# Pair 14's second product moved into the last first product, the last SwiGLU by halves, the softmax's VectorE operations pinned in program order

## The chip, the core and the metric

The kernel runs on one core of one Trainium2 chip, as one launch. The core has TensorE (PE: matmuls and transposes, with its weight loads listed as PEld), VectorE (DVE), ScalarE (ACT), GpSimd (POOL) and SyncE (SP), which here issues nearly all loads. The metric is the device time of one execution in microseconds; a lower one is better. [...]

## What is computed

One encoder block on 256 positions of 1024 columns, in float32. The first half (adaLN modulation, gated delta rule, short convolution, output projection) is untouched by the change. The second half is a mixture of 32 experts, four for each token, and a final RMSNorm:

```
h = rmsnorm(x, norm2_w) * (1 + sc_f) + sh_f
logits = h @ router_w + router_b
top_val, top_idx = lax.top_k(logits, 4);  gates = softmax(top_val)
for each expert e, on the tokens that chose it:
    gate, up = split(x_blk @ w1[e] + b1[e])            # 1024 -> 2 * 1024
    act = min(gate, 7) * sigmoid(1.702 * gate) * (clip(up, -7, 7) + 1)
    y = act @ w2[e] + b2[e]                            # 1024 -> 1024
x = x + gt_f * sum over the four experts of gates * y
out = rmsnorm(x, final_norm_w)
```

## The kernel before

**Routing.** The logits `lg` of 128 tokens by two halves go through VectorE: `max` and `match_replace` give the selection `sel` (copied four times wide into `sel4`). Three small matmuls of TensorE count, for every token, its rank among an expert's tokens; `rk` (L1280) is made of them, and `slots_of(0)` (L1312) turns `rk` into the 0/1 matrix `P` of the first four experts. `gather_part` multiplies `P` with the normalised tokens (`h2h` and `h2l`, two parts of one number) and writes the experts' inputs, `XT`, 128 columns at a time. `busy(n)` issues matmuls whose result nobody reads. `route_counts()`, called behind the first product of pair 0 in the program, makes `sel4`, the counts and the order of the other 28 experts, and the softmax of the gates (`nmx`, `ex`, `den`, `gat`, L1492 to L1498).

**The stream of experts.** The 32 experts are taken as 8 groups of four, and each group as two pairs: pairs 0 to 15. The first product of a pair (`w1_pair`) has eight chunks k0 to k7; a chunk is two loads of 1 MB (one for each expert of the pair) and 16 matmuls, in four column quarters c of 512 into four PSUM banks: c = 0, 1 are the gate's halves, c = 2, 3 the up's. Profile rows count each such matmul as two records, so a chunk is 32 of them. `swiglu(128, pss[half], pss[2 + half])` works on quarters (0, 2), then on (1, 3): g = min, tanh on ScalarE, u = clip, and two fused operations on VectorE; the tile `g` has two buffers, `u` and `th` one each. `to_ff` turns its result by eight transposes and two ScalarE copies into `aT`. The second product is a `Second` object with four blocks of the same size (two loads of 1 MB, 32 records), and `end()`: VectorE scales the two PSUM banks into `ysb`, and two `combine` calls, each of two matmuls, add the rows back to the tokens' `x1`.

Pair p's loop step runs its first product, and then the four blocks of pair p - 1 with `turn(p)`, the transposes of pair p, among them. The combines of pair p - 1 run within the first product of pair p + 1. In the last step (p = 15) blocks 0 and 1 of pair 14 run inside the first product, behind k2 and k4, and blocks 2 and 3 behind k7. Then come the combines of pair 14 and the second product of pair 15 in another shape, `w2_cols`: columns 0 to 767 in four steps (loads of 768 KB), the first parts of the final norm, and columns 768 to 1023. `xf`, `square` and `finish_part` are the final RMSNorm.

**Order.** A scheduler puts each engine's instructions in order by a simulated timeline. Instructions marked `pin(...)` (`tc.keep_in_program_order`) keep their order in the program among the pinned ones of their engine; all of the expert stage's matmuls and transposes are pinned (`held[0]`). The weight loads go through one ring of 18 half-slots of 1 MB (`w_half`); six chunks of pair 0 and three of pair 1 are loaded ahead, k6 and k7 of pair 0 into tiles that are free till later (`pre`). SP issues a load when the half-slot is released by the matmuls that read it.

## Time and profile before

| | us |
|---|---|
| median of 3 runs | 1378.63 (1376.73 to 1378.85) |
| the profiled execution, its own time | 1378.51 |
| its span, first to last instruction | 1376.7 |
| TensorE busy | 1268.5 (92%) |
| VectorE busy | 516.8 (38%) |
| ScalarE busy | 282.2 (21%) |

The profile's page gives busy time and shares over the whole span; the stages differ, so the rows below take them apart. A timeline row gives the start, the time, the engine, the line, the operation with output and inputs, the count of merged instructions, and in brackets the idle time of the engine before it with what ended that. The chain that the page follows back from the end reaches only to 1367.9 us, where the runtime branch for overflowing experts ends, and so it says nothing of the stages ahead of that.

### The profile page before, as it was taken

Reading aid. Unit: us, or ns where it says so; the run is one execution under the profiler, and the core shown is the slowest. Engines: PE = TensorE matmul, PEld = TensorE weight load, DVE = VectorE, ACT = ScalarE, POOL = GpSimd, SP = SyncE. Lnnn points to the kernel's source line nnn. Section 1 sums busy time; section 2 is a strip of 40 time slices with the busy share of each in tenths; the row PEclk is TensorE's granted clock in tenths of the full one; section 3 lists DMA queues with packets and bytes.
Section 4 is the critical chain, followed back from the end, with each engine's and each line's share of the span. In section 5 each row is a group of like instructions: output and inputs, shape, how many; then the busy total and the mean of one; then the engine's idle time right before and its main releaser. Section 6 shows DMA issues by size and latency. Waiting matters only on the chain. (4 is left out here: it accounts for less than half of the span.)

```text
span 1376.7 us, 24562 instructions
## 1 busy us (share of the span) xinstructions
PE 1268.5 (92%) x10276; PEld 666.0 (48%) x10277; DVE 516.8 (38%) x1018; ACT 282.2 (21%) x546; POOL 151.9 (11%) x126
## 2 busy tenths in 40 slices
PE   6999998899999999999999898988989898898986
PEld 4888897899996333223333233322322332232322
DVE  3387879965773321232122112122211212211113
ACT  3455562554642010101001001000100100010001
POOL 4555785000100000000000000000000000000000
PEclk9999999999999999999999999999999999999998
DMA  9978977246697899999999999999999999999994
GB/s 338 309 234 270 309 234 239 77 146 251 224 369 291 365 421 421 414 421 421 421 420 421 421 420 421 420 421 421 420 421 421 420 420 421 421 420 421 421 400 172
DMA packets 132533, 492.69 MB, mean 358 GB/s; under 512 B 10942, under 2 KB 66623, under 8 KB 84801
## 3 DMA queue, kind: packets, MB, share of 16 engines
q1 hardware_dynamic: 128176, 485.95, 89.4%
q10 hardware_dynamic: 4241, 5.12, 1.1%
q8 instruction: 82, 1.34, 0.4%
q14 instruction: 34, 0.28, 0.1%
HBM read 486.82 MB, written 4.21 MB: 357 GB/s over the span
## 5 line engine op out<-in xcount | busy, mean ns | idle before, releaser
L1303 PE MATMUL acc<-wst,XT 128*32 128x512 f32 x4088 | 474.9, 596 | 24.3 <-DMA wst<-in_moe_w_dram 24.3
L1303 PEld LDWEIGHTS acc<-wst,XT 128*32 128x32 f32 x4088 | 133.0, 110 | 339.4 <-issue 281.7
L1303 PE MATMUL acc<-wst,aT 128*32 128x512 f32 (+1 forms) x2112 | 250.5, 585 | 25.6 <-DMA wst<-in_moe_w_dram 25.6
L313 PE MATMUL mm<-hh,wl 128*128 128x256 f32 (+1 forms) x520 | 149.9, 289 | 6.2 <-DVE wl L263 3.7
L1303 PEld LDWEIGHTS acc<-wst,aT 128*32 128x32 f32 x2112 | 70.5, 110 | 175.8 <-issue 113.3
L311 PE MATMUL mm<-hh,wh 128*128 128x256 f32 (+1 forms) x520 | 151.7, 292 | 1.2 <-DVE cacc L556 1.2
L312 PE MATMUL mm<-hl,wh 128*128 128x256 f32 (+1 forms) x520 | 149.9, 288 | 0.0
L262 ACT CAST wh<-raw 128x1024 fp32r<-128x1024 f32 (+1 forms) x89 | 91.9, 1039 | 95.1 <-PE mm L312 52.2
L1360 DVE TENSOR_SCALAR g<-acc 128x512 f32<-128x512 f32 x32 | 22.1, 692 | 229.8 <-PE acc L1303 229.5
L88 POOL TENSOR_TENSOR rs<-ss,half_m 128x2 f32<-128x2 f32 x3 | 2.1, 701 | 949.6 <-DVE ss L1752 884.9
L311 PEld LDWEIGHTS mm<-hh,wh 128*128 128x128 f32 (+1 forms) x520 | 100.6, 194 | 12.6 <-issue 8.3
L313 PEld LDWEIGHTS mm<-hh,wl 128*128 128x128 f32 (+1 forms) x520 | 100.5, 193 | 8.6 <-DVE wl L263 3.9
L312 PEld LDWEIGHTS mm<-hl,wh 128*128 128x128 f32 (+1 forms) x520 | 100.7, 194 | 0.9 <-issue 0.8
L263 POOL TENSOR_TENSOR wl<-raw,wh 128x1024 fp32r<-128x1024 f32 x36 | 88.5, 2468 | 71.3 <-ACT wh L262 64.3
L1361 ACT ACTIVATE th<-g 128x512 f32<-128x512 f32 x32 | 20.2, 630 | 362.6 <-DVE g L1360 297.4
L1407 DVE TENSOR_TENSOR x<-x,misc 128x512 f32<-128x512 f32 (+1 forms) x66 | 44.3, 672 | 124.8 <-PE misc L1303 124.8
L1414 DVE TENSOR_TENSOR ysb<-acc,gtf 128x512 f32<-128x512 f32 (+1 forms) x33 | 22.2, 675 | 137.1 <-PE acc L1303 137.1
L263 DVE TENSOR_TENSOR wl<-raw,wh 128x1024 fp32r<-128x1024 f32 (+1 forms) x53 | 64.0, 1212 | 24.0 <-ACT wh L262 23.9
L1303 PE MATMUL misc<-ysb,pgT 128*128 128x512 f32 (+1 forms) x132 | 64.0, 606 | 1.8 <-DVE ysb L1414 1.0
L1332 DVE TENSOR_SCALAR XT<-misc,afc,mod 128x256 f32<-128x256 f32 x32 | 17.4, 544 | 127.1 <-PE misc L1303 127.1
L1303 PE MATMUL misc<-P,h2h 128*128 128x256 f32 x128 | 39.6, 332 | 20.5 <-ACT XT L1334 18.4
L1303 PEld LDWEIGHTS misc<-P,h2h 128*128 128x128 f32 x128 | 24.0, 187 | 53.2 <-issue 27.5
(390 smaller groups left out, 1384.9 us busy)
## 6 DMA issues: line engine op xcount, KB each, us to landing
wst<-in_moe_w_dram SPq DMA_DIRECT2D x372, 1024.0 KB, 19.8
raw<-in_w_in_dram SPq DMA_DIRECT2D x36, 1024.0 KB, 7.4
raw<-in_ada_w_dram SPq DMA_DIRECT2D x24, 1024.0 KB, 9.6
wst<-in_moe_w_dram SPq DMA_DIRECT2D x8, 768.0 KB, 19.0
raw<-in_w_out_sc_dram SPq DMA_DIRECT2D x4, 1024.0 KB, 5.2
raw<-in_w_up_a_dram SPq DMA_DIRECT2D x4, 1024.0 KB, 8.6
raw<-in_w_o_dram SPq DMA_DIRECT2D x4, 1024.0 KB, 10.2
wst<-in_moe_w_dram SPq DMA_DIRECT2D x16, 256.0 KB, 6.6
```

The lines of the kernel that those rows point to most:

```text
L88: G.tensor_tensor(dst, src, half_m.to_broadcast([128, n]), op=OP.pow)
L262: a = A.copy(wh, src)
L263: b = (V if job.lo == "v" else G).tensor_tensor(wl, src, wh.bitcast(FT), op=OP.subtract)
L311: PE.matmul(ps, wh[:, k, :], ah[:, k, :], start=k == 0, stop=False, skip_group_check=True)
L312: PE.matmul(ps, wh[:, k, :], al[:, k, :], start=False, stop=False, skip_group_check=True)
L313: PE.matmul(ps, wl[:, k, :], ah[:, k, :], start=False, stop=k == KT - 1, skip_group_check=True)
L1303: return held[0](PE.matmul(*a, **kw))
L1332: V.tensor_scalar(xq[:, k], o, afc[:, k:k + 1], mod[:, 24 + k:25 + k], op0=OP.mult, op1=OP.add)
L1360: V.tensor_scalar(g[:n], g_ps[:n], 7.0, None, op0=OP.min)
L1361: A.activation(th[:n], g[:n], AF.Tanh, scale=0.851)
L1407: V.tensor_tensor(xv, xv, p[:, 0:n], op=OP.add)
L1414: V.tensor_tensor(y, ps[:, 0:n], gtf_box[0][:, c0:c0 + n], op=OP.mult)
```

## The change

Four edits. The column quarters of every first product run in the order 0, 2, 1, 3. Five kinds of VectorE operations of `route_counts` (the copies of `sel4`, the two products with the sum for `den`, the reciprocal, the two for `gat`) are pinned. In the last step, all four blocks of pair 14 run inside the first product, behind k2, k3, k4 and k5; its scaling follows block 3, and its two combines stand behind k6. `to_ff` can do one half, so that pair 15's first half is turned ahead of `w2_cols` and its second half behind the first column step.

```diff
-            for c in range(4):
+            for c in (0, 2, 1, 3):
                 for j in range(4):
                     mm(pss[c][j * 32:(j + 1) * 32], xq[:, k, (4 * pa + j) * 32:(4 * pa + j + 1) * 32],
...
-    def to_ff(gs):
-        aT = work.tile([128, KT, 128], FT, name="aT", tag="aT", bufs=2)
-        for half in range(2):
+    def to_ff(gs, aT=None, halves=(0, 1)):
+        if aT is None:
+            aT = work.tile([128, KT, 128], FT, name="aT", tag="aT", bufs=2)
+        for half in halves:
...
-            V.tensor_copy(sel4[:, t, 1:4], sel4[:, t, 0:1].to_broadcast([128, 3, NE]))
+            pin(V.tensor_copy(sel4[:, t, 1:4], sel4[:, t, 0:1].to_broadcast([128, 3, NE])))
...
-            V.scalar_tensor_tensor(ex[:, t], ex[:, t], 1.0, sel[:, t], op0=OP.mult, op1=OP.mult,
-                                   accum_out=den[:, t:t + 1])
-        V.reciprocal(den, den)
+            pin(V.scalar_tensor_tensor(ex[:, t], ex[:, t], 1.0, sel[:, t], op0=OP.mult, op1=OP.mult,
+                                       accum_out=den[:, t:t + 1]))
+        pin(V.reciprocal(den, den))
         for t in range(2):
-            V.tensor_scalar(gat[:, t], ex[:, t, None, :].to_broadcast([128, 4, NE]), den[:, t:t + 1], None, op0=OP.mult)
+            pin(V.tensor_scalar(gat[:, t], ex[:, t, None, :].to_broadcast([128, 4, NE]), den[:, t:t + 1], None,
+                                op0=OP.mult))
...
-        done = 0
         if p == NP - 1:
 
             box = []
-            for done, k in enumerate((2, 4)):
-                at[k].append(lambda c=done: (box or box.append(second(p - 1)) or box)[0].block(c))
-            done += 1
+            at[2].append(lambda: box.append(second(p - 1)))
+            for c in range(4):
+                at[2 + c].append(lambda c=c: box[0].block(c))
+            at[5].append(lambda: box.extend(box[0].end()))
+            at[6] += [lambda h=h: box[1 + h]() for h in range(2)]
         first_product(p, at)
...
-        if p:
+        if 0 < p < NP - 1:
...
-            at[3 if done else 2].append(lambda: turn(p))
-            sp = box[0] if done else second(p - 1)
-            for c in range(done, 4):
+            at[2].append(lambda: turn(p))
+            sp = second(p - 1)
+            for c in range(4):
...
-    last = (aTs[NP - 1], gts[NQ - 1], regs[NQ - 1])
-    sums[NP - 2][0]()
-    w2_cols(NP - 1, PARTS[0:2], *last, {0: [sums[NP - 2][1]]})
+    last = (to_ff(gs[NP - 1], None, (0,)), gts[NQ - 1], regs[NQ - 1])
+    w2_cols(NP - 1, PARTS[0:2], *last, {0: [lambda: to_ff(gs[NP - 1], last[0], (1,))]})
```

## Rows read from the trace of the kernel before

**Rows 1.** Windows: length, busy us (instructions) by engine, clock, DMA share, GB/s.
```profile
439.30:441.80 2.50, 2.50 (x24) 1.08 (x24) 0.00 (x0) 0.56 (x1) 0.00 (x0) 1.00 0.35 79
...
471.60:476.80 5.20, 5.20 (x52) 1.56 (x48) 2.31 (x11) 0.00 (x0) 0.00 (x0) 1.00 0.21 54
476.80:1338.00 861.20, 790.49 (x6332) 262.84 (x6324) 187.92 (x396) 59.12 (x102) 0.10 (x1) 1.00 1.01 420
```

**Rows 2.** Timeline of VectorE, routing.
```profile
429.23 0.41 DVE L1474 COPY sel<-sel 128x96 f32<-128x96 f32 x2
430.77 0.19 DVE L1494 SCALAR_TENSOR_TENSOR ex<-ex,sel 128x32 f32<-128x32 f32 x1 [1.13 <-ACT ex L1493]
...
431.81 0.22 DVE L1280 SCALAR_TENSOR_TENSOR rk<-misc,sel 128x64 f32<-128x64 f32 x1
432.13 0.76 DVE L1312 TENSOR_TENSOR P<-iota,rk 128x256 fp32r<-128x256 f32 x2
432.81 2.46 DVE L1214 SCALAR_TENSOR_TENSOR h2l<-x,rs,h2h 128x256 fp32r<-128x256 f32 x6
...
444.59 0.54 DVE L1332 TENSOR_SCALAR XT<-misc,afc,mod 128x256 f32<-128x256 f32 x1 [8.86 <-PE misc L1303]
```

**Rows 3.** Timeline of TensorE, routing and the start of pair 0.
```profile
429.20 0.39 PE L1277 MATMUL misc<-sel,tri_s 128*128 128x32 f32 x2
429.42 1.14 PE L1185 MATMUL mm<-one_f,ident 128*128 128x128 f32 x8
432.71 0.36 PE L1303 MATMUL misc<-P,h2h 128*128 128x256 f32 x1 [2.15 <-DVE P L1312]
...
434.46 5.17 PE L1303 MATMUL acc<-wst,XT 128*32 128x512 f32 x32
...
440.24 3.64 PE L1303 MATMUL acc<-wst,XT 128*32 128x512 f32 x32
```

**Rows 4.** Windows, columns as in rows 1: the first chunk of pair 0.
```profile
434.40:437.70 3.30, 3.30 (x17) 0.79 (x20) 1.33 (x4) 0.00 (x0) 0.00 (x0) 0.51 1.02 393
```

**Rows 5.** Timeline of SP's queue: weight issues near pairs 0 and 1.
```profile
439.68 0.84 SPq L968 DMA_DIRECT2D wst<-in_moe_w_dram  x2
...
474.62 4.24 SPq L1428 DMA_DIRECT2D wst<-in_moe_w_dram  x4
```

**Rows 6.** Timeline of TensorE, from the last first product's k7.
```profile
1328.10 3.20 PE L1303 MATMUL acc<-wst,XT 128*32 128x512 f32 x26 [1.34 <-DMA wst<-in_moe_w_dram]
...
1333.09 3.64 PE L1303 MATMUL acc<-wst,aT 128*32 128x512 f32 x32 [0.51 <-DMA wst<-in_moe_w_dram]
1338.05 3.62 PE L1303 MATMUL acc<-wst,aT 128*32 128x512 f32 x26 [1.32 <-DMA wst<-in_moe_w_dram]
1341.60 1.22 PE L1306 MATMUL misc<-ident,g 128*128 128x128 f32 x8
1343.03 1.98 PE L1303 MATMUL misc<-ysb,pgT 128*128 128x512 f32 x4 [0.21 <-ACT aT L1398]
1344.95 2.79 PE L1303 MATMUL acc<-wst,aT 128*32 128x512 f32 x32
...
1349.58 7.95 PE L1303 MATMUL acc<-wst,aT 128*32 128x512 f32 x96
```

**Rows 7.** Timeline of VectorE and ScalarE: the last SwiGLU and `aT`.
```profile
1329.20 0.69 DVE L1360 TENSOR_SCALAR g<-acc 128x512 f32<-128x512 f32 x1 [35.28 <-PE acc L1303]
...
1330.92 0.69 DVE L1362 TENSOR_SCALAR u<-acc 128x512 f32<-128x512 f32 x1 [0.17 <-PE acc L1303]
...
1332.44 0.69 DVE L1364 SCALAR_TENSOR_TENSOR g<-th,g 128x512 f32<-128x512 f32 x1
...
1342.38 1.09 ACT L1398 ACTIVATE aT<-misc 128x512 f32<-128x512 f32 x2 [8.53 <-PE misc L1306]
```

**Rows 8.** Timeline of TensorE: two longer waits within the stream.
```profile
906.53 3.64 PE L1303 MATMUL acc<-wst,aT 128*32 128x512 f32 x32 [1.78 <-DMA wst<-in_moe_w_dram]
...
1031.82 5.15 PE L1303 MATMUL acc<-wst,aT 128*32 128x512 f32 x28 [2.42 <-DMA wst<-in_moe_w_dram]
```

## The prediction

> **What bounds the kernel now.** I read the windows by stage first, then the timelines of the two places that the change touches, and last the waits of TensorE. In the windows [rows 1] the reader is to see three facts. From 476.8 us to 1338 us the DMA engines are full at 420 GB/s while TensorE is busy 790 of 861 us: the weight stream sets the pace there, and TensorE work that moves about inside this stretch is worth nothing. Just ahead of it the stream twice runs dry, from 439.3 to 441.8 us and from 471.6 to 476.8 us (DMA share 0.35 and 0.21) with TensorE at 100%. By the code the ring of 18 half-slots is then full of weights (six chunks of pair 0, three of pair 1), and SP can issue only when TensorE has finished a chunk. So whatever starts pair 0 sooner moves the whole stream. After 1338.05 us no matmul waits for a weight any more (the tail, below): the rest of the kernel is a chain of TensorE, VectorE and ScalarE, which sets the end.

> **Routing: the held operations.** The timeline of VectorE [rows 2] shows what stands ahead of pair 0. The rank counts for `rk` leave TensorE at 429.20 + 0.39 = 429.59 us [rows 3], but `rk` starts at 431.81 us. Ahead of it VectorE copies `sel4` (from 429.23 us), then stands 1.13 us for ScalarE's exponentials, then does the softmax from 430.77 us. None of that is needed by `rk`, `P` or the gather; it is needed by the matmuls after pair 0. TensorE stands 2.15 us for `P` [rows 3]. The change pins those operations, which puts them behind `P` and the `h2l` columns that are pinned ahead of them. Then `rk` can start when its counts are there, which I take at 0.2 us after 429.59, an estimate from the 0.2 us between `P`'s first half, half of 0.76 us from 432.13 on, and the gather at 432.71. With the row's spacings, `rk` to `P` 0.32 us and `P` to gather 0.58 us, the gather starts at 429.79 + 0.32 + 0.58 = 430.69 us and not at 432.71: 2.02 us sooner. It can't be sooner than the end of the warm-up matmuls, 429.42 + 1.14 = 430.56 [rows 3], so 2.15 is the upper bound. The lower bound is nothing, if other work slips into VectorE's freed place.

> The held operations, seven instructions and two accumulator reads, take 0.41 us for `sel4` and about 1.04 us for the softmax [rows 2]. I cost them at nothing: behind `P` come `h2l` (2.46 us), then they, then the second `XT` eviction (0.54), done at about 430.86 + 2.46 + 1.45 + 0.54 = 435.3 us. What waits for it is the second chunk of pair 0, which would start near 436.7. So 1.4 us of cover; past that, each us late is a us on TensorE. After that VectorE stands 8.86 us [rows 2].

> **Routing: the clock.** [...] The first chunk of pair 0 therefore takes 5.17 us where the next takes 3.64 [rows 3]. With the gap gone I take it at 3.64: another 1.53 us. Bounds: 0 (the clock falls all the same) to 1.53.

> **What becomes of these 3.55 us.** SP's first issue of the stage, at 439.68 us, waits for that first chunk; the one at 474.62 us waits for the first chunk of pair 1 [rows 5]. With TensorE 3.55 us sooner, the first issue comes at 436.1, while the earlier transfers still run (to 439.3): the first dry stretch goes. The second starts some 2 us sooner for it and ends 3.55 us sooner, with TensorE's release. From there the full stream [rows 1] and all behind it run 3.55 us ahead. These us can only be lost again after the last weight of the stream.

> **The tail.** Moved are blocks 1 to 3 of pair 14's second product (six 1 MB loads and 96 matmul records): block 1 from behind k4 to behind k3, blocks 2 and 3 from behind k7 to behind k4 and k5. On SP, k4's loads come behind block 1's, and those of k6 and k7 behind blocks 2 and 3. Twelve chunks of 2 MB go ahead of pair 15's second-product weights either way, so the eleventh and the twelfth still land when they do now, at 1333.09 and 1338.05 [rows 6], only they are k6 and k7 and no longer blocks 2 and 3. No queue but SP's is passed, and SP's other waits don't change, the ring being as deep.

> From 1333.09 us on I count TensorE's work. Now: two blocks, eight transposes, two combines, four column steps, ending at 1349.58 + 7.95 = 1357.53 [rows 6]: 24.44 us, of which it stands 1.32 (for the weights) and 0.21 us. Afterwards: k6, two combines, k7, four transposes, one column step, four transposes, three column steps. A chunk of either product is 32 records of 3.64 us, so it is the same work, and only the idle time differs. The combines take 1.92 us each (1343.03 to 1344.95): k7 starts at 1333.09 + 3.55 + 3.84 = 1340.5, after its weights, so the 1.32 us go. (With k7 at 1338.05 the combines would have been free; they are not.)

> What comes instead is the last SwiGLU, which today runs under blocks 2 and 3 and afterwards has nothing over it but k7 itself. With S the start of k7, today's rows give the first half's `g` at S + 1.10 and the third quarter's `u` at S + 2.82, 0.86 us a quarter [rows 6, 7]. In the order 0, 2, 1, 3 the first half's `u` is in the second quarter: S + 1.96. From `u` to the end of its last operation is 1332.44 + 0.69 - 1330.92 = 2.21 us, so half 0 is ready at S + 4.17; its transposes start near S + 4.25, where k7 ended at S + 3.55: 0.70 us idle. ScalarE starts 0.78 us after the transposes (1341.60 to 1342.38) and takes 0.55, so the first column step starts near S + 5.75; less 0.61 us of transposes that is 0.87 us idle. Half 1, four more operations of about 0.7 us, is ready near S + 7.0, under that step. New idle 1.57 us against 1.53: **the tail comes out even, at +0.04 us.** Bounds: -1.53 (no idle at all), and +0.86 if VectorE takes the second `g` ahead of the two operations that finish half 0.

> The quarters' new order in the other pairs, 4 x 4 matmuls either way, costs and brings nothing: their SwiGLU ends long before its transposes, under the full stream.

> [...] The row at 1031.82 us shows TensorE after 2.42 us without work at the lower clock, 5.15 us for 28 records; after 1.78 us at 906.53 it kept 3.64 [rows 8]. In the new tail it would stand 0.70 and 0.87 us with four transposes between. [...]

> **Sum.** -2.02 - 1.53 + 0.04 = -3.51 us. The profiled execution took 1378.51 us with a span of 1376.7, so 1375.0; the median of the runs is 0.12 us above it: **1375.1 us**, 0.26% less. About 0.2% (2.8 us) is what a measurement of this kernel can tell from no change.

> **Rivals.** (1) *The clock falls in pair 0 all the same.* For it: the small matmuls from 428 to 430.6 us stay. Against: the only standstill there is gone. 1376.6 us. [...] (3) *Combines and SwiGLU both hide:* 1373.6. Against: the times of k7 above. (4) *Slower: the last SwiGLU stands bare.* If VectorE does both halves before TensorE gets the first, the transposes wait till S + 7.1 in place of 4.25: +2.85 us, and as after the shorter gaps of [rows 3, 8] the clock falls: +1.53. Net +0.87 us, 1379.5. It decides from 3.51 us of extra time on. For it: `g`, `u`, `th` are few buffers, and today VectorE does both `g` first [rows 7]. Against: today the second `g` is ready ahead of the first `u`; in the new order it isn't.

> **Chances.** Forecast 0.54, (1) 0.14, (2) 0.17, (3) 0.06, (4) 0.09. Faster than by 0.2% means under 1375.9: most of the forecast (0.47, since runs spread over 2 us), all of (3), a little of (1) and (2): 0.56. Slower by 0.2%, over 1381.4, is only the worst of (4) or something that I don't see: 0.07. Within: 0.37. The range goes from (3) with some spread, 1372.9, to (2) with the second `g` first and spread, 1378.6; above lies (4).

> **What would show it.** Gather near 430.7 us; the first chunk of pair 0 in 3.6 us at full clock; no dry stretch near 440; k7 of pair 15 starting some 2.4 us after its weights; two short idle times before the first column step, together near 1.6 us, and the clock through them. It is wrong if `rk` still waits for something on VectorE, if the clock falls in either place, or if the end of the stream doesn't move with pair 0.

## The result and the profile after

The changed kernel takes 1385.32 us (median of 5 runs, 1383.42 to 1387.48), the kernel before 1377.57 us (5 runs, 1376.73 to 1378.85): a ratio of 1.0054, 95% interval 1.0042 to 1.0067. The forecast was 1375.1 us, 0.26% less; it came out 0.54% more. The profiled execution took 1385.25 us with a span of 1383.4, 6.7 us above the span before.

Where are they? The first place to look is TensorE's waits between 424 and 560 us, each with its sum, count and longest in us. Of the changed kernel:

```profile
PE misc L1303 <- DVE sel L1475: 4.5, 1, 4.5
PE misc L1303 <- ACT XT L1334: 2.6, 4, 0.7
PE misc L1303 <- DVE P L1312: 2.1, 1, 2.1
```

The second and third are the waits of before: the one for `P`, which was to go, is still 2.1 us. The first is new. VectorE's timeline of the changed kernel shows both reasons:

```profile
426.55 0.15 DVE L1493 TENSOR_SCALAR nmx<-mx 128x1 f32<-128x1 f32 x1
...
427.44 0.87 DVE L1214 SCALAR_TENSOR_TENSOR h2l<-x,rs,h2h 128x256 fp32r<-128x256 f32 x2
429.76 0.19 DVE L1495 SCALAR_TENSOR_TENSOR ex<-ex,sel 128x32 f32<-128x32 f32 x1 [1.45 <-ACT ex L1494]
...
430.81 0.22 DVE L1280 SCALAR_TENSOR_TENSOR rk<-misc,sel 128x64 f32<-128x64 f32 x1
431.13 0.76 DVE L1312 TENSOR_TENSOR P<-iota,rk 128x256 fp32r<-128x256 f32 x2
...
471.06 0.69 DVE L1364 SCALAR_TENSOR_TENSOR g<-th,g 128x512 f32<-128x512 f32 x1
471.67 0.40 DVE L1475 COPY sel<-sel 128x96 f32<-128x96 f32 x2
```

Against [rows 2], the softmax has not moved: it still stands ahead of `rk` and still waits for ScalarE's exponentials, 1.45 us in place of 1.13, since the copies no longer fill a part of that time. That `rk` still stands behind something on VectorE is the first of the prediction's own signs of being wrong. Only the copies into `sel4` have moved, and not behind `P` but 40 us further, behind the last operation of pair 0's SwiGLU. The first small matmuls of `route_counts`, the counts that TensorE runs behind pair 0's first product, read them. TensorE's timeline of the changed kernel:

```profile
431.70 0.36 PE L1303 MATMUL misc<-P,h2h 128*128 128x256 f32 x1 [2.15 <-DVE P L1312]
...
433.52 5.11 PE L1303 MATMUL acc<-wst,XT 128*32 128x512 f32 x32
...
471.97 1.06 PE L1303 MATMUL misc<-sel,one_f 128*128 128x32 f32 x4 [4.50 <-DVE sel L1475]
...
474.64 2.09 PE L119 MATMUL acc<-b1c,tri_ul 32*128 32x512 f32 x8
476.66 7.46 PE L1303 MATMUL acc<-wst,XT 128*32 128x512 f32 x64
484.05 0.63 PE L1303 MATMUL misc<-perm,rT 32*128 32x32 f32 x4
```

The same stretch of the kernel before:

```profile
468.44 0.63 PE L1303 MATMUL misc<-sel,one_f 128*128 128x32 f32 x4
...
469.88 1.14 PE L119 MATMUL acc<-b1c,tri_ul 32*128 32x512 f32 x8
470.96 7.07 PE L1303 MATMUL acc<-wst,XT 128*32 128x512 f32 x64
477.96 0.63 PE L1303 MATMUL misc<-perm,rT 32*128 32x32 f32 x4
```

The reader is to see two losses. TensorE stands 4.50 us. And what follows is slower: from the counts to the `perm` matmuls (the next small ones, behind two chunks of pair 1) 12.08 us (471.97 to 484.05) against 9.52 us (468.44 to 477.96), 2.56 us more. The windows of the changed kernel (columns as in [rows 1]) say why: TensorE's granted clock, given as a share of its full speed, falls within the wait (1.00 up to 470 us, 0.50 from 471 us), and the stream, which pair 1's first chunk has to restart, stands dry meanwhile (DMA share 0.02):

```profile
467.50:472.00 4.50, 0.03 (x1) 0.03 (x1) 3.61 (x7) 1.26 (x2) 0.00 (x0) 0.85 0.79 328
472.00:476.70 4.70, 4.70 (x24) 2.80 (x26) 1.91 (x13) 0.63 (x2) 0.00 (x0) 0.50 0.02 3
```

The tail is where it was expected. TensorE's timeline of the changed kernel from k6 of pair 15 on, and VectorE's of the last SwiGLU:

```profile
1339.36 3.63 PE L1303 MATMUL acc<-wst,XT 128*32 128x512 f32 x28 [1.33 <-DMA wst<-in_moe_w_dram]
1342.92 3.89 PE L1303 MATMUL misc<-ysb,pgT 128*128 128x512 f32 x8
1346.74 3.64 PE L1303 MATMUL acc<-wst,XT 128*32 128x512 f32 x32
1351.47 0.74 PE L1306 MATMUL misc<-ident,g 128*128 128x128 f32 x4 [1.09 <-DVE g L1364]
1352.90 2.79 PE L1303 MATMUL acc<-wst,aT 128*32 128x512 f32 x32 [0.69 <-ACT aT L1399]
1355.62 0.75 PE L1306 MATMUL misc<-ident,g 128*128 128x128 f32 x4
1356.30 7.95 PE L1303 MATMUL acc<-wst,aT 128*32 128x512 f32 x96
```

```profile
1348.73 0.69 DVE L1362 TENSOR_SCALAR u<-acc 128x512 f32<-128x512 f32 x1 [0.17 <-PE acc L1303]
1349.53 0.69 DVE L1363 SCALAR_TENSOR_TENSOR g<-u,g 128x512 f32<-128x512 f32 x1
1350.13 0.68 DVE L1360 TENSOR_SCALAR g<-acc 128x512 f32<-128x512 f32 x1
1350.73 0.68 DVE L1364 SCALAR_TENSOR_TENSOR g<-th,g 128x512 f32<-128x512 f32 x1
```

From 1339.36 to 1356.30 + 7.95 = 1364.25 us it takes 24.89 us, against 24.44 in [rows 6]: +0.45 us. The sum of the 6.7 us: the gather starts 1.01 us sooner in this execution, from work ahead of the change; 7.10 us are lost between gather and `perm` matmuls (484.05 - 431.70 against 477.96 - 432.71); 0.18 us more by the eleventh chunk of the last step (k6 in the changed kernel, block 2 in the one before: 1339.36 and 1333.09, less the 6.09 us of offset at the `perm` matmuls); 0.45 in the tail.

### The profile page after: what moved, and what is told of

Read it like the earlier page. It is cut to its first block, busy times and chain, and to the rows that moved or that the text cites. A ratio compares the mean times of both kernels' runs of the same rounds, so it can differ in the third digit from the quotient of the medians.

```text
span 1383.4 us, 24553 instructions
## 1 busy us (share of the span) xinstructions
PE 1271.6 (92%) x10276; PEld 667.9 (48%) x10277; DVE 512.7 (37%) x1018; ACT 282.0 (20%) x546; POOL 152.0 (11%) x126
## 5 line engine op out<-in xcount | busy, mean ns | idle before, releaser
L1303 PE MATMUL acc<-wst,aT 128*32 128x512 f32 (+1 forms) x2112 | 253.8, 587 | 25.7 <-DMA wst<-in_moe_w_dram 25.0
L556 DVE SCALAR_TENSOR_TENSOR cacc<-mm,col,cacc 128x254 f32<-128x254 f32 (+1 forms) x96 | 46.0, 480 | 10.0 <-ACT cacc L553 7.9
```

The source lines that it names most:

```text
L556: V.scalar_tensor_tensor(a[:, o0:o1], p[:, s0:s1], cw(j), a[:, o0:o1], op0=OP.mult, op1=OP.add)
L1303: return held[0](PE.matmul(*a, **kw))
```

## The experiments

Theory A: the pin ties an instruction behind whatever was traced just before it on its engine, which for the `sel4` copies is pair 0's last SwiGLU operation; this wait and the clock behind it are the whole loss. Theory B: the moved second product costs it. Theory C: the new order of the quarters delays every pair.

**One pin undone** (changed kernel):

```diff
-            pin(V.tensor_copy(sel4[:, t, 1:4], sel4[:, t, 0:1].to_broadcast([128, 3, NE])))
+            V.tensor_copy(sel4[:, t, 1:4], sel4[:, t, 0:1].to_broadcast([128, 3, NE]))
```

> The changed kernel with one pin undone, that of the two copies into sel4; all else as changed (quarter order, blocks and combines in the last first product, last SwiGLU by halves, the softmax's pins). Theory A (the pin ties the copies behind the last SwiGLU operation of pair 0, and TensorE's counts wait for them): the 4.50 us wait and the low clock behind it go, the stream's end comes back by about 7.1 us, and only the tail's +0.45 us stays: about 0.5 us above the kernel before, ratio 1.000. Theory B (the moved second product costs it) and theory C (the new quarter order delays every pair): the time stays near 1385 us.

Measured: 1379.3 us against 1378.64 for before on the same chip, ratio 1.0004 (0.9995 to 1.0013). The softmax, still pinned here, still starts ahead of `rk` (431.23 and 432.27 us): its pins hold nothing. The counts follow pair 0 without a wait, as TensorE's timeline shows:

```profile
468.83 0.63 PE L1303 MATMUL misc<-sel,one_f 128*128 128x32 f32 x4
...
471.34 7.07 PE L1303 MATMUL acc<-wst,XT 128*32 128x512 f32 x64
```

**That pin alone** (kernel before): the reverse edit.

> The kernel before with that one pin alone, on the two copies into sel4. Theory A: about 7 us slower than before (ratio 1.005), with the same wait of 4 to 5 us ahead of the counts and the clock at its lower level for some 6 us. Theories B and C: as before, ratio 1.000.

Measured: 1385.89 us, ratio 1.0059 (1.0044 to 1.0075), with the old tail and the old order of the quarters:

```profile
472.43 0.63 PE L1303 MATMUL misc<-sel,one_f 128*128 128x32 f32 x4 [4.50 <-DVE sel L1474]
...
476.61 8.65 PE L1303 MATMUL acc<-wst,XT 128*32 128x512 f32 x64
485.19 0.63 PE L1303 MATMUL misc<-perm,rT 32*128 32x32 f32 x4
```

The two together settle the place: the pin on two copies, which take 0.4 us together, brings the whole loss. B and C fall: with that pin gone, all else that was changed costs at most 0.13% (the upper end of the first interval).

**The operations really held behind the slots** (kernel before, with edges to the last `h2l` operation in place of pins):

```diff
+            h2l_box[:] = [pin(V.scalar_tensor_tensor(h2l[:, t, cs], ...))]
...
-            V.tensor_copy(sel4[:, t, 1:4], sel4[:, t, 0:1].to_broadcast([128, 3, NE]))
+            with tc.issue_after(h2l_box[0].ins):
+                V.tensor_copy(sel4[:, t, 1:4], sel4[:, t, 0:1].to_broadcast([128, 3, NE]))
...
-            V.scalar_tensor_tensor(ex[:, t], ex[:, t], 1.0, sel[:, t], op0=OP.mult, op1=OP.mult,
-                                   accum_out=den[:, t:t + 1])
+            with tc.issue_after(h2l_box[0].ins):
+                V.scalar_tensor_tensor(ex[:, t], ex[:, t], 1.0, sel[:, t], op0=OP.mult, op1=OP.mult,
+                                       accum_out=den[:, t:t + 1])
```

> The kernel before with the copies into sel4 and the softmax's products queued behind the last h2l operation by edges to that operation, which is what the prediction took the pins to do; the tail is as before. The prediction's routing terms are tried here: the gather 2.0 us sooner and the first chunk of pair 0 at full clock, -1.5 us: 3.5 us less than before, ratio 0.9975. Rival: the clock falls at pair 0 all the same: -2.0 us, ratio 0.9985. If the time of pair 0's start does not reach the end of the stream: ratio 1.000.

Measured: 1375.04 us against 1378.64, ratio 0.9977 (0.9968 to 0.9986): 3.6 us. VectorE's timeline, then TensorE's:

```profile
429.57 0.23 DVE L1282 SCALAR_TENSOR_TENSOR rk<-misc,sel 128x64 f32<-128x64 f32 x1 [0.31 <-PE misc L1279]
429.90 0.76 DVE L1314 TENSOR_TENSOR P<-iota,rk 128x256 fp32r<-128x256 f32 x2
430.57 2.46 DVE L1216 SCALAR_TENSOR_TENSOR h2l<-x,rs,h2h 128x256 fp32r<-128x256 f32 x6
432.95 0.41 DVE L1477 COPY sel<-sel 128x96 f32<-128x96 f32 x2
```

```profile
429.37 1.14 PE L1185 MATMUL mm<-one_f,ident 128*128 128x128 f32 x8
430.47 0.36 PE L1305 MATMUL misc<-P,h2h 128*128 128x256 f32 x1
...
432.13 3.64 PE L1305 MATMUL acc<-wst,XT 128*32 128x512 f32 x32
```

The gather follows the warm-up matmuls without a gap, the first chunk takes 3.64 us and not 5.17, and the stream no longer stands dry near 440 us (the DMA share is 0.96 or more in every microsecond from 434 to 444 us).

**The wait filled**, to tell idle time and clock apart: matmuls that nobody reads, between pair 0's last chunk and the counts. On the changed kernel, 20 matmuls of 128 columns:

```diff
         if p == 0:
+            fp = misc()
+            for _ in range(20):
+                mm(fp[:, 0:128], ident, one_f, start=True, stop=True, skip_group_check=True)
             turned.extend(route_counts())
```

> The changed kernel with 20 matmuls that nobody reads put on TensorE between pair 0's last chunk and the counts, to keep it at work through the wait (about 4.3 us of the 4.5). It tells the two parts of the loss apart. Theory A with the clock as second part: the wait is as long, the clock stays at 1.00, and 2.6 us of the 7.1 come back: about 1382.7 us. If the low clock costs nothing of its own: as the changed kernel, 1385.3 us.

Measured: 1385.34 us (4 executions), ratio 1.0053 (1.0038 to 1.0068). The profiled execution kept the clock at 1.00 through the filling and the counts (in every microsecond from 436 to 517 us) and took 1382.53 us, as theory A has it; the other three, of which there is no trace, took 1385.3 to 1386.1. Next, four matmuls of 512 columns on `h2h`:

> The changed kernel with four matmuls of 512 columns on the tokens' data, which nobody reads, between pair 0's last chunk and the counts (about 3.8 us of the 4.5), with more rounds than e5_fill, whose one profiled execution kept the clock and took 1382.5 us while its other executions took 1385.3 to 1386.1. If the low clock behind the wait costs its 2.6 us: 1382.7 us against the changed kernel's 1385.3, ratio to before 1.003. If not: 1.0053.

Measured: 1385.8 us, ratio 1.0049 (1.0035 to 1.0063): a miss. Again the trace has no low clock at the counts (1.00 in every microsecond from 467 to 477 us); but this execution lost the clock in the new tail (0.50 from 1352 to 1354 us; rows below). So the same filling went onto the kernel before with the one pin, which has the old tail:

> The kernel before with the pin on the sel4 copies and the same four unread matmuls of 512 columns in TensorE's wait; the tail is that of before, so that the clock of the new tail, which fell in the profiled executions of e6_hold_tail and e8_fill_data (1.7 us) and not in three others, can't blur the answer. If the low clock behind the wait costs time of its own, the loss of e2_sel4_only (7.2 us, ratio 1.0059) shrinks to the wait, 4.6 us: ratio 1.0033. If it costs nothing in most executions: 1.005 to 1.006 again.

Measured: 1382.59 us against 1378.28, ratio 1.0028 (1.0017 to 1.0038), where the pin alone gave 1.0059. The wait is as long (0.88 us behind 3.70 us of filling), the rows behind it are back to 0.63 and 1.14 us at a clock of 1.00 (in every microsecond from 465 to 485 us), and from the counts to the `perm` matmuls (at 483.04 us) it is 9.52 us, as in the kernel before:

```profile
468.94 3.70 PE L1303 MATMUL misc<-h2h 128*128 128x512 f32 x8
473.52 0.63 PE L1303 MATMUL misc<-sel,one_f 128*128 128x32 f32 x4 [0.88 <-DVE sel L1474]
...
474.96 1.14 PE L119 MATMUL acc<-b1c,tri_ul 32*128 32x512 f32 x8
```

So the wait itself costs some 4.3 us (1382.59 - 1378.28). The pin without the filling cost 7.25 us (1385.89 - 1378.64), so the low clock behind the wait cost about 2.9 us (each time against the kernel before on its own chip). The traces have 2.56 us for it in the changed kernel and 3.24 us in the kernel with the pin alone (472.43 to 485.19, 12.76 us, against 9.52).

**Both parts as they were meant**: the edges above and the tail as changed.

> The changed kernel with the pins replaced by the edges of the kernel e4_hold: the routing as the prediction meant it, and the tail as changed. If the two parts add up: -3.5 us from the routing, +0.45 us from the tail: 3.1 us less than before, ratio 0.9978. [...]

Measured: 1375.8 us against 1378.85, ratio 0.9978 (0.9969 to 0.9987). The size is as added up. Its profiled execution shows a fall of the clock in the tail (0.50 from 1343 to 1346 us), and so does that of the second filling (0.50 from 1352 to 1354 us); TensorE's timelines, first this kernel, then that one:

```profile
1341.25 0.74 PE L1308 MATMUL misc<-ident,g 128*128 128x128 f32 x4 [1.09 <-DVE g L1366]
1342.68 4.47 PE L1305 MATMUL acc<-wst,aT 128*32 128x512 f32 x32 [0.69 <-ACT aT L1401]
```

```profile
1349.29 0.74 PE L1306 MATMUL misc<-ident,g 128*128 128x128 f32 x4 [1.10 <-DVE g L1364]
1350.72 4.48 PE L1303 MATMUL acc<-wst,aT 128*32 128x512 f32 x32 [0.69 <-ACT aT L1399]
```

The same step takes 2.79 us in the changed kernel's trace, where the clock stays at 1.00: 1.7 us.

**The second combine in the tail's idle times.** Of pair 14's two combines the first stays behind k6; the second is split by token halves, one behind k7 and one behind the first half's transposes. (`combine` takes the token halves as an argument for this; that part of the edit is left out here.)

```diff
-            at[6] += [lambda h=h: box[1 + h]() for h in range(2)]
+            at[6].append(lambda: box[1]())
...
+    box[2]((0,))
     last = (to_ff(gs[NP - 1], None, (0,)), gts[NQ - 1], regs[NQ - 1])
+    box[2]((1,))
```

> The kernel e6_hold_tail with the second combine of pair 14 taken from behind k6 and put into the two idle times of the new tail: its first token half behind k7, its second behind the first half's transposes. The tail's account says: k7 starts 1.9 us sooner, 0.5 us after its weights, and the 1.8 us idle are filled: 1.7 us less than e6_hold_tail, 4.8 us less than before, ratio 0.9965. Rival: VectorE's adds for the moved combine fall among the SwiGLU's operations and push half 0 back by as much (0.7 to 1.4 us): ratio 0.997 to 0.998.

Measured: 1374.15 us (1373.63 to 1374.78) against 1378.85, ratio 0.9964 (0.995 to 0.9977): the lowest median of all, 4.7 us below the kernel before, though its interval overlaps those of the edges alone and of the edges with the changed tail. TensorE's timeline:

```profile
1329.76 3.63 PE L1305 MATMUL acc<-wst,XT 128*32 128x512 f32 x28 [1.35 <-DMA wst<-in_moe_w_dram]
1333.32 1.98 PE L1305 MATMUL misc<-ysb,pgT 128*128 128x512 f32 x4
1335.23 3.64 PE L1305 MATMUL acc<-wst,XT 128*32 128x512 f32 x32
1338.81 1.13 PE L1305 MATMUL misc<-ysb,pgT 128*128 128x512 f32 x2
1339.97 0.74 PE L1308 MATMUL misc<-ident,g 128*128 128x128 f32 x4
1341.16 1.12 PE L1305 MATMUL misc<-ysb,pgT 128*128 128x512 f32 x2 [0.45 <-DVE x L1410]
...
1345.62 7.95 PE L1305 MATMUL acc<-wst,aT 128*32 128x512 f32 x96
```

From k6 to the end of the column steps it is 1345.62 + 7.95 - 1329.76 = 23.81 us, 1.08 less than as changed and not the 1.7 expected: VectorE's add for the moved combine stands behind SwiGLU operations, and TensorE waits 0.45 us for it; and the combine in two parts takes 0.3 us more (1.16 and 1.06 us from row to row, against 1.91 in one). The rival had the adds push half 0 back; its last operation ends at 1339.91 us, 4.68 us after k7's start, as without them (4.67), so it is not that. The same tail without the routing edges:

> The kernel before with the tail of e7_hold_gap alone (quarter order, blocks in the last first product, SwiGLU by halves, the second combine in the idle times; no routing edges or pins). By the account of the tail: 1.2 us less than before, ratio 0.9991, against about +0.5 us for the tail as changed (e1_sel4_free, 1.0004). If the tail as changed loses by a clock that falls in part of the executions and by nothing else, filling the idle times takes that away too: nearer 0.9985.

Measured: 1377.88 us against 1378.28, ratio 0.9996 (0.9987 to 1.0005). Its trace has 23.79 us for that stretch, 0.65 less than before and not the 1.2 expected; the interval holds that, and no change too.

## Why the prediction was wrong, step by step

**The step that failed** is "The change pins those operations, which puts them behind `P` and the `h2l` columns". The description of a pin ahead of the prediction, as an order among the pinned instructions of an engine, was wrong: in the changed kernel the pinned softmax runs at 429.76 us, ahead of `rk` at 430.81, which is pinned too and stands earlier in the program. The placements are those of an edge to the one instruction that was traced just before on the same engine, and to nothing else; no run shows the scheduler's edges themselves, so this is read from where the instructions stand. (The pins are on four kinds of operations, as the list ahead of the prediction has them, and not on five.) `route_counts` is traced behind pair 0's first product. So the copies, its first VectorE instructions, were tied to the end of pair 0's SwiGLU; the softmax's product is traced behind `nmx`, which is free and early (426.55 us), and the pinned reciprocal and `gat` behind that product, so that their edges held nothing. The gain of 3.55 us therefore did not come, and a wait of 4.50 us with 2.56 us of low clock did. A routing gain of nothing stood in the prediction as a bound, for another reason ("nothing, if other work slips into VectorE's freed place"). No rival had an operation arriving too late for its reader, and a time over 1381.4 us had a chance of 0.07, in part for "something that I don't see": "needed by the matmuls after pair 0" was written down, and what stands just ahead of those matmuls on VectorE was not looked up.

**The routing terms** were right for the edit that they described. With real edges the gather comes at 430.47 us (430.69 forecast, in an execution that runs 0.05 us ahead at the warm-up matmuls), the first chunk takes 3.64 us, and the total falls by 3.6 us (3.55). The clock stands at 1.00 there in every microsecond from 425 to 485 us; in the changed kernel, where TensorE still stands 2.15 us for `P`, it is 0.53 from 433.4 to 436.7 us, and the first chunk takes 5.11 us.

**That the gain reaches the end of the stream** held both ways: the 7.1 us lost and the 3.6 us won at pairs 0 and 1 both stand at the end.

**The tail** was right in mechanism and nearly in size: k7 2.4 us behind its weights (1346.74 against 1339.36 + 4.96, the spacing of the last two loads in [rows 6]), two idle times of 1.09 and 0.69 us against 0.70 and 0.87, +0.45 us against +0.04. Of the 0.41 us of difference 0.21 is more idle time. VectorE took the second `g` ahead of the operation that finishes half 0, as the named bound has it, and that operation ended at S + 4.67 us and not at S + 4.17; the second idle time had been put 0.17 us above what its own terms add up to (4.25 + 0.78 + 0.55 = 5.58, not 5.75). The other 0.20 us is a term that was put at nothing: eight transposes in one group take 1.22 us, in two groups 0.74 and 0.68.

**The clock in the tail** fell, but not in every execution: of five profiled executions with this tail, two show it (0.50, the first column step 1.7 us longer), and three keep 1.00. The chance of 0.17 for (2) and the upper end of the range, 1378.6 us, count on such a fall; no run shows the time that was put on it there, and what the runs show is 4.47 and 4.48 us against 2.79 in those two executions. These are one execution each of five kernels with the same tail, so that no kernel has two traces that differ: whether the clock in the tail of one kernel differs from execution to execution is not shown.

**Open** is how often the clock falls there in executions without a trace, and why the two fillings on the changed kernel left its median where it was, although their traces show the clock kept at the counts and the four matmuls of 512 columns on the old tail brought back 2.9 us. The mean clock on record for the three executions of the first filling without a trace, 0.987 to 0.993, is within that of the kernel before (0.987 to 0.995) and does not tell.

## What to carry to other kernels

An ordering mark has to be read as the edge that it draws: ask which instruction is the other end, and where that one may float. When an operation is moved later, look up its first reader and what stands ahead of it on its own engine by then; two copies, 0.4 us together, cost 7 us because the next matmuls of the critical engine read them. Where a stretch of work is moved off the end, the idle time that it leaves is the place for what else was to be done: the combine in front of k7 cost what it saved, the combine in the gaps gained 1.1 us in the traces (the intervals of the times overlap).
